# Layer 1's q and k turned by DMA in two 16-bit planes instead of on TensorE

## The chip, the cores and the metric

The kernel runs on one core of a Trainium2 chip. The metric is the time of one execution on the device in microseconds. A core has TensorE (PE: matmuls, and transposes as matmuls with an identity), VectorE (DVE), ScalarE (ACT), GpSimd (POOL), SyncE (SP), which here does nothing but issue DMAs, and 16 DMA engines. TensorE reads its operands from the on-chip memory SBUF and writes to the eight banks of PSUM; ScalarE and VectorE bring results from there into SBUF. Each engine runs its own instructions strictly in their order and waits at semaphores for the others.

## The reference

A decoder of two layers over 256 tokens with 2048 features in 32-bit floats. Each layer adds a mixer and a SwiGLU network (hidden size 5632) to the residual, each behind an RMS norm; a last norm ends it. Layer 0's mixer is sliding-window attention beside an mLSTM; layer 1's is forgetting attention with 16 heads of 128, and the change lies there:

```python
def forgetting_attention_mixer(xn, w_in, b_f, w_out):
    proj = xn @ w_in
    q, k, v, f = split_cols(proj, FOX_SIZES)
    ...
    log_f = jax.nn.log_sigmoid(f.astype(jnp.float32) + b_f.astype(jnp.float32))
    c = jnp.transpose(jnp.cumsum(log_f, axis=1), (0, 2, 1))
    ...
        s = jnp.einsum('bhqd,bhkd->bhqk', qb, k, preferred_element_type=jnp.float32) * scale
        s = s + cb[..., None] - c[:, :, None, :]
        s = jnp.where(pb[:, None] >= k_pos[None, :], s, -jnp.inf)
        p = jax.nn.softmax(s, axis=-1)
        return jnp.einsum('bhqk,bhkd->bhqd', p.astype(v.dtype), v)
    ...
    return out @ w_out
```

## The kernel before

**Projections.** Products keep 32-bit accuracy by splitting: each 32-bit value is a rounded part `hi` and a remainder `lo`, and three matmuls (hi·hi, lo·hi, hi·lo; L192 to L194) add up in PSUM. The activations lie split and transposed in SBUF (`xh`, `xl`: 16 blocks of 128 features by 256 tokens). The weights come in chunks of 256 rows by 512 columns (512 KB): SP loads a chunk into one of four `raw` buffers (L105), ScalarE rounds it into one of six `hi` buffers (L161), VectorE subtracts into one of six `lo` buffers (L162), and TensorE runs 12 matmuls on it. `project` (through `gemm`) walks the eight chunks of 512 output columns and leaves two PSUM banks, one for each block of 128 tokens (`acc`).

**Layer 1's attention** treats the 16 heads in four groups of four (`for i in range(4)`). For each group it projects q, then k, then v. Behind each projection `nat1` (L865) scales the two banks by the norm's factor into an SBUF tile of tokens by features (`qk`, one buffer, for q and k; `vn` for v). The scores need q and k the other way round, features on the partitions. So `transpose_many` turns the eight 128x128 blocks of a q or a k on TensorE, four to a PSUM bank (tile `ptm`, L306), and VectorE copies each bank into `qt` or `kt` (L307). Then `attention` runs: scores (L316, L323), bias and mask on VectorE, the exponentials on ScalarE (L345), the transposes of the weights (L366, L370), and the products with v (L374, L375).

**Order.** A planner simulates the program and lays down each engine's order, with the program's order as priority; so the matmuls of the next projection fill the time in which a softmax runs on the other engines. Work that is to be issued late goes into the list `later` as a pair of a step and a function: `gemm` calls `run_due` after the split of each chunk, with the chunk's number as the step, and what is due is issued there, on ScalarE behind that chunk's `hi` cast (`issue_after`).

**Turning by DMA.** The kernel has this step in two places already. A DMA transpose takes 16-bit elements, so the lower and the upper halves of the 32-bit words are copied apart by ScalarE into two planes, each plane is turned by two DMA transposes (one for each block of 128 tokens, 128 by 512 elements) from the SP queue, and two ScalarE copies put the halves together again: `split_turned` for the residual (planes L272, transposes L274, joins L279) and the end of a block of the FFN (L521, L523, L528), whose join is due some chunks later.

Of the kernel before, what the change touches and what calls it, by code (L numbers as in the profile page):

```python
# [10 lines left out]
U16 = mybir.dt.uint16  # L11
# [6 lines left out]
P = 128  # L18
D = 2048
S = 256  # L20
NT = S // P
KT = D // P
FF = 5632
NB = 512
# [15 lines left out]
}  # L40
MID = 6
MID_DOWN = 5
LATER = (6, 10)
LATER_DOWN = (5, 6)
RAWS = 4
# [10 lines left out]
def trunk(  # L56
# [20 lines left out]
    nc = tc.nc  # L77
# [89 lines left out]
    def new_acc():  # L167
        return [pa.tile([P, NB], F32, tag="acc", name="acc") for _ in range(NT)]

    later = []  # L170
# [6 lines left out]
    def gemm(acc, lhs, w, c0, n, k_from, k_to, k_all, skew=1, step=0):  # L177
        k0 = k_from
        while k0 < k_to:
            last = k_to == k_all and k0 + skew * CK >= k_all  # L180
            chunks = [load_chunk(w, kc, c0, n) for kc in range(k0, k_all if last else k0 + CK, CK)]
            run_due(later, step + k0 // CK)
            order = [(i, t) for i in range(len(chunks) * CK) for t in range(NT)]
            if last:
                order.sort(key=lambda it: it[1])
            for i, t in order:
                k = k0 + i
                hi, lo = (c[:, i % CK, 0:n] for c in chunks[i // CK])
                ah, al = lhs(k)
                ts = slice(t * P, (t + 1) * P)  # L190
                o = acc[t][:, 0:n]
                nc.tensor.matmul(o, ah[:, ts], hi, start=(k == 0), stop=False)  # L192
                nc.tensor.matmul(o, ah[:, ts], lo, start=False, stop=False)  # L193
                nc.tensor.matmul(o, al[:, ts], hi, start=False, stop=(k == k_all - 1))  # L194
            k0 += len(chunks) * CK
# [7 lines left out]
    def project(w, c0, n):  # L203
        acc = new_acc()
        gemm(acc, x_of, w, c0, n, 0, KT, KT)
        return acc
# [61 lines left out]
    def split_turned(idx, n, flat, turned, extra=None):  # L268
        planes = flat.bitcast(U16).rearrange("p (b t n) -> p b t n", b=2, t=NT)
        hu = h[:, :, n * NB : (n + 1) * NB].bitcast(U16).rearrange("p t (n b) -> p t n b", b=2)  # L270
        for b in range(2):
            nc.scalar.copy(planes[:, b, :, :], hu[:, :, :, b])  # L272
            for t in range(NT):
                nc.sync.dma_start_transpose(turned[:, b, :, t, :], planes[:, b, t, :])  # L274

        def join():
            ju = flat.bitcast(U16).rearrange("p (n b) -> p n b", b=2)
            for b in range(2):
                nc.scalar.copy(ju[:, :, b], turned[:, b, :, :, :].rearrange("p k t q -> p (k t q)"))  # L279
            split_scaled(idx, n, extra, flat.rearrange("p (k s) -> p k s", k=4))  # L280

        return join

    def scrap(fp, n):
        if n == 0:
            box = fp.tile([P, 4, NB], F32, tag="c", name="box", bufs=1)
            halves = box[:, 0:2, :], box[:, 2:4, :]
        else:
            halves = [fp.tile([P, CK, NB], F32, tag="raw", name="box", bufs=RAWS) for _ in range(2)]
        flat, turned = (a.rearrange("p a n -> p (a n)") for a in halves)  # L290
        return flat, turned.bitcast(U16).rearrange("p (b k t q) -> p b k t q", b=2, t=NT, q=P)
# [10 lines left out]
    def transpose_many(dst, srcs):  # L302
        m = len(srcs)
        pt = pm.tile([P, 4, P], F32, tag="pm", name="ptm")
        for i, s_ in enumerate(srcs):
            nc.tensor.transpose(pt[:, i, :], s_, ident)  # L306
        nc.vector.tensor_copy(dst, pt[:, 0:m, :])  # L307
# [78 lines left out]
    def out_proj(w, idx, key, extra):  # L386
        last = KT - 4
        for n0 in (0, 2):
# [3 lines left out]
            for i in range(2):  # L392
                gemm(accs[i], m_of, w, (n0 + i) * NB, NB, last, KT, KT, step=6)
                add_out(accs[i], n0 + i)
                if n0 == 0:
                    later.append((LATER[i], split_turned(idx, i, *scrap(extra[2], i), extra)))
                else:
# [75 lines left out]
    def ffn(layer, fp, sx, sd, key, idx_next=None, key_next=None, finish=None):  # L473
# [6 lines left out]
        for g0, g1 in zip(PARTS, PARTS[1:]):  # L480
# [4 lines left out]
            for g in range(g0, g1):  # L485
# [58 lines left out]

                todo = [(MID if g < g1 - 1 else MID_DOWN, join)]

# [314 lines left out]
    with tc.tile_pool(name="od", bufs=1) as od:  # L861
        def nat1(acc, n, name, bufs=1):
            t_ = od.tile([P, NT, n], F32, tag=name, name=name, bufs=bufs)
            for t in range(NT):
                nc.scalar.mul(t_[:, t, :], acc[t][:, 0:n], r1[:, t : t + 1])  # L865
            return t_

        VT = 2 * FD
        c_v = 2 * FOX_H * FD
        acc = project(wi1, c_v + 14 * FD, VT + FOX_H)  # L870
        fg = od.tile([P, NT, FOX_H], F32, name="fg")
        for t in range(NT):
            nc.vector.scalar_tensor_tensor(
                out=fg[:, t, :],
                in0=acc[t][:, VT : VT + FOX_H],
                scalar=r1[:, t : t + 1],
                in1=bias_f,
                op0=ALU.mult,
                op1=ALU.add,
            )  # L880
        vtail = nat1(acc, VT, "vtail")
        nl = od.tile([P, NT, FOX_H], F32, name="nl")
        nc.scalar.activation(nl, fg, AF.Abs)
        nc.scalar.activation(nl, nl, AF.Exp, scale=-1.0)
        nc.scalar.activation(nl, nl, AF.Ln, bias=1.0)
        nc.vector.scalar_tensor_tensor(out=nl, in0=fg, scalar=0.0, in1=nl, op0=ALU.min, op1=ALU.subtract)
        nc.vector.tensor_scalar(nl, nl, -1.0, None, op0=ALU.mult)
        pc = pm.tile([P, NB], F32, tag="pm", name="pcf")
        nc.tensor.matmul(pc[:, 0:FOX_H], upper, nl[:, 0, :], start=True, stop=True)
        nc.tensor.matmul(pc[:, FOX_H : 2 * FOX_H], ones, nl[:, 0, :], start=True, stop=False)  # L890
        nc.tensor.matmul(pc[:, FOX_H : 2 * FOX_H], upper, nl[:, 1, :], start=False, stop=True)
        negc = od.tile([P, NT, FOX_H], F32, name="negc")
        nc.vector.tensor_copy(negc.rearrange("p t h -> p (t h)"), pc[:, 0 : 2 * FOX_H])
        pr = pm.tile([P, NB], F32, tag="pm", name="prf")
        nc.tensor.matmul(pr[0:FOX_H, 0:P], nl[:, 0, :], upper, start=True, stop=True)
        nc.tensor.matmul(pr[0:FOX_H, P:S], nl[:, 0, :], ones, start=True, stop=False)
        nc.tensor.matmul(pr[0:FOX_H, P:S], nl[:, 1, :], upper, start=False, stop=True)
        negct = od.tile([FOX_H, S], F32, name="negct")
        nc.vector.tensor_copy(negct, pr[0:FOX_H, 0:S])
        scratch = dp.tile([FOX_H, S], F32, name="scratch")  # L900
        nc.gpsimd.dma_start(scratch, negct)
        cb1 = od.tile([P, FOX_H, S], F32, name="cb1")
        nc.gpsimd.dma_start(cb1, scratch.partition_broadcast(P))
        cb0 = od.tile([P, FOX_H, P], F32, name="cb0")
        for dst, src in ((cb0, cb1[:, :, 0:P]), (cb1[:, :, P:S], cb1[:, :, P:S])):
            nc.gpsimd.affine_select(
                out=dst, in_=src, pattern=[[0, FOX_H], [-1, P]], compare_op=ALU.is_ge, fill=NEG, base=0, channel_multiplier=1
            )

        for i in range(4):  # L910
            qt = od.tile([P, 4, S], F32, tag="qt", name="qtf")
            kt = od.tile([P, 4, S], F32, tag="kt", name="ktf")
            for off, dst in ((0, qt), (FOX_H * FD, kt)):
                n_ = nat1(project(wi1, off + i * NB, NB), NB, "qk")
                for g in range(0, 4, 2):
                    transpose_many(
                        dst[:, g : g + 2, :].rearrange("p g (t q) -> p (g t) q", q=P),
                        [n_[:, t, (g + u) * FD : (g + u + 1) * FD] for u in range(2) for t in range(NT)],
                    )
            vn = nat1(project(wi1, c_v + i * NB, NB if i < 3 else VT), NB if i < 3 else VT, "vn")  # L920

            def v_of(j, b, i=i, vn=vn):
                if i == 3 and j >= 2:
                    return vtail[:, b, (j - 2) * FD : (j - 1) * FD]
                return vn[:, b, j * FD : (j + 1) * FD]

            attention(
                od,
                lambda j, b, qt=qt: qt[:, j, b * P : (b + 1) * P],
                lambda j, kt=kt: kt[:, j, :],  # L930
                v_of,
                FD,
                FD**-0.5,
                cb0[:, 4 * i : 4 * i + 4, :],
                cb1[:, 4 * i : 4 * i + 4, :],
                4 * i,
                negc=negc[:, :, 4 * i : 4 * i + 4],
            )
# [76 lines left out]
```

## Time and profile before

| | |
|---|---|
| median of 3 runs | 2132.01 us (2131.75 to 2132.25) |
| the profiled execution | 2131.7 us |
| its span, first to last instruction | 2130.0 us |
| TensorE matmuls busy | 2113.6 us (99%) |
| VectorE busy | 1666.1 us (78%) |
| ScalarE busy | 1256.1 us (59%) |
| DMA, hardware queue of SP | 61.5% of 16 engines' time |
| granted TensorE clock, mean | 0.998 |

The profile comes from one execution. An engine's busy time is the union of its instructions; matmuls overlap in the pipeline, so the row of a group gives a matmul's length, and the distance between the starts of two neighbours gives what one costs. A group's row reads: line, engine, operation, the tile written and the tiles read, shape, count, then total and mean time and the idle time before it with what ended it. In a row of one line or tile the durations are shortest, median and longest in ns, then the first and the last start in us. In a row of the order of time the first number is the start, the second the length. `PEld` is TensorE's weight load, `SPq` an instruction in SP's queue.

### The profile page before, as it was taken

What the parts mean: (1) busy time and instruction counts of PE and PEld (TensorE: products, weight loads), DVE (VectorE), ACT (ScalarE), POOL (GpSimd) and SP (SyncE); (2) the same over time, 40 slices, a digit from 0 to 9 for tenths busy, and PEclk for the clock granted to TensorE, in tenths of its full rate; (3) what the DMA queues carried; (4) which work ended last, traced back from release to release, by engine and by line L of the source; (5) the groups of instructions that cost most, each with busy time, mean ns of one, the idle gap of its engine ahead of it and who ended that gap; (6) DMA issues with size and microseconds to landing.
All of it is one profiled execution on the core that took longest, in us unless ns stands there. A gap on an engine that the chain in (4) does not pass through costs nothing.

```text
span 2130.0 us, 26773 instructions
## 1 busy us (share of the span) xinstructions
PE 2113.6 (99%) x9732; PEld 1755.0 (82%) x9732; DVE 1666.1 (78%) x2116; ACT 1256.1 (59%) x1584; POOL 39.6 (2%) x61
## 2 busy tenths in 40 slices
PE   8999999999999999999999999999999999999998
PEld 7888888888888888888888888888888888888886
DVE  6665558998899988998755554579998998889984
ACT  6565457765567646666645544576654667556753
POOL 2010000000000000000010000000000000000000
PEclk9999999999999999999999999999999999999999
DMA  8444547665667666766575564675756666656763
GB/s 268 149 150 148 169 150 265 217 208 197 198 207 225 211 207 193 235 206 198 163 235 168 168 178 142 195 247 187 238 188 208 207 208 206 228 189 208 228 200 125
DMA packets 267941, 421.47 MB, mean 198 GB/s; under 512 B 67136, under 2 KB 75424, under 8 KB 267552
## 3 DMA queue, kind: packets, MB, share of 16 engines
q1 hardware_dynamic: 267136, 416.02, 61.5%
q0 software_dynamic: 624, 3.72, 0.5%
q8 instruction: 76, 1.25, 0.2%
q14 instruction: 57, 0.47, 0.1%
q10 hardware_dynamic: 48, 0.02, 0.0%
HBM read 404.48 MB, written 2.11 MB: 191 GB/s over the span
## 4 chain that ended last, share of the span: by engine, by line
PE 98%; ACT 1%; issue 0%; DMA 0%; DVE 0%; DVEq 0%; POOLq 0%; POOL 0%; ACTq 0%
PE acc L402 17%; PE acc L403 17%; PE acc L404 17%; PE acc L192 10%; PE acc L193 10%; PE acc L194 10%; PE prod L402 4%; PE prod L404 4%; PE prod L403 4%; PE p L323 1%; PE ptm L306 1%; PE po L374 1%; PE pt L245 0%; PE pp L366 0%; PE p L316 0%
## 5 line engine op out<-in xcount | busy, mean ns | idle before, releaser
L161 ACT CAST hi<-raw 128x1024 fp32r<-128x1024 f32 (+1 forms) x692 | 705.1, 1033 | 667.3 <-PE acc L404 314.4
L162 DVE TENSOR_TENSOR lo<-raw,hi 128x1024 fp32r<-128x1024 f32 (+1 forms) x692 | 821.5, 1200 | 314.7 <-ACT hi L161 312.9
L403 PE MATMUL acc<-lo,xh 128*128 128x512 f32 x946 | 368.1, 389 | 0.0
L404 PE MATMUL acc<-hi,xl 128*128 128x512 f32 x946 | 367.2, 389 | 0.0
L402 PE MATMUL acc<-hi,xh 128*128 128x512 f32 x946 | 366.5, 389 | 0.0
L192 PE MATMUL acc<-hi,xh 128*128 128x512 f32 (+3 forms) x736 | 276.7, 377 | 0.8 <-ACT hi L161 0.8
L194 PE MATMUL acc<-hi,xl 128*128 128x512 f32 (+3 forms) x736 | 276.8, 377 | 0.0
L193 PE MATMUL acc<-lo,xh 128*128 128x512 f32 (+3 forms) x736 | 276.3, 375 | 0.0
L404 PEld LDWEIGHTS acc<-hi,xl 128*128 128x128 f32 x946 | 177.6, 188 | 36.9
L403 PEld LDWEIGHTS acc<-lo,xh 128*128 128x128 f32 x946 | 177.6, 188 | 36.7
L402 PEld LDWEIGHTS acc<-hi,xh 128*128 128x128 f32 x946 | 177.6, 188 | 36.6
L295 DVE TENSOR_TENSOR lt<-t,ht 128x1024 fp32r<-128x1024 f32 x168 | 199.7, 1217 | 3.6 <-ACT ht L294 3.6
L403 PE MATMUL acc<-lo,mh 128*128 128x512 f32 x514 | 200.2, 389 | 0.0
L402 PE MATMUL acc<-hi,mh 128*128 128x512 f32 x514 | 200.0, 389 | 0.0
L404 PE MATMUL acc<-hi,ml 128*128 128x512 f32 x514 | 198.5, 389 | 0.0
L294 ACT CAST ht<-t 128x1024 fp32r<-128x1024 f32 x168 | 174.8, 1052 | 20.8 <-PE acc L404 12.8
L192 PEld LDWEIGHTS acc<-hi,xh 128*128 128x128 f32 x736 | 139.0, 189 | 25.0 <-ACT hi L161 1.2
L194 PEld LDWEIGHTS acc<-hi,xl 128*128 128x128 f32 x736 | 139.1, 189 | 24.4 <-issue 0.8
L193 PEld LDWEIGHTS acc<-lo,xh 128*128 128x128 f32 x736 | 139.2, 189 | 24.0 <-issue 0.7
L192 PE MATMUL acc<-hi,mh 128*128 128x512 f32 x320 | 125.2, 391 | 1.2 <-ACT mh L294 1.2
L193 PE MATMUL acc<-lo,mh 128*128 128x512 f32 x320 | 125.3, 392 | 0.0
L194 PE MATMUL acc<-hi,ml 128*128 128x512 f32 x320 | 123.9, 390 | 0.0
(311 smaller groups left out, 2779.4 us busy)
## 6 DMA issues: line engine op xcount, KB each, us to landing
raw<-in_w_gate_dram SPq DMA_DIRECT2D x176, 512.0 KB, 4.3
raw<-in_w_up_dram SPq DMA_DIRECT2D x176, 512.0 KB, 4.6
raw<-in_w_down_dram SPq DMA_DIRECT2D x176, 512.0 KB, 4.6
raw<-in_w_in_odd_dram SPq DMA_DIRECT2D x88, 512.0 KB, 3.8
raw<-in_w_in_even_dram SPq DMA_DIRECT2D x64, 512.0 KB, 4.0
raw<-in_w_out_even_dram SPq DMA_DIRECT2D x32, 512.0 KB, 3.6
raw<-in_w_out_odd_dram SPq DMA_DIRECT2D x32, 512.0 KB, 4.2
raw<-in_w_in_odd_dram SPq DMA_DIRECT2D x8, 272.0 KB, 2.9
```

The lines of the kernel that those rows point to most:

```text
L161: latest[0] = nc.scalar.copy(hi[:, :, 0:n], raw[:, :, 0:n])
L162: nc.vector.tensor_tensor(out=lo[:, :, 0:n], in0=raw[:, :, 0:n], in1=hi[:, :, 0:n].bitcast(F32), op=ALU.subtract)
L192: nc.tensor.matmul(o, ah[:, ts], hi, start=(k == 0), stop=False)
L193: nc.tensor.matmul(o, ah[:, ts], lo, start=False, stop=False)
L194: nc.tensor.matmul(o, al[:, ts], hi, start=False, stop=(k == k_all - 1))
L294: nc.scalar.copy(dst_h, src)
L295: nc.vector.tensor_tensor(out=dst_l, in0=src, in1=dst_h.bitcast(F32), op=ALU.subtract)
L306: nc.tensor.transpose(pt[:, i, :], s_, ident)
L323: nc.tensor.matmul(p1[:, jj, :], q_of(j, 1), k_of(j), start=True, stop=True)
L402: nc.tensor.matmul(o, ah, hi, start=start, stop=False)
L403: nc.tensor.matmul(o, ah, lo, start=False, stop=False)
L404: nc.tensor.matmul(o, al, hi, start=False, stop=stop)
```

## The change

For the groups 0, 1 and 2, q and k are turned by the DMA step: the new function `turn` copies the two planes of the `qk` tile on ScalarE, issues four DMA transposes on SP, and returns a function `join`, which copies the two turned planes into `qt` or `kt` on ScalarE. The join is put into `later` with step 6 (`AHEAD`): for a q it is issued behind the cast of the seventh chunk of the k projection, for a k behind that of the seventh chunk of the v projection. Group 3 keeps its transposes on TensorE. `planes` and `turned` are new tiles with one buffer each, 4 KB a partition each.

```diff
+AHEAD = 6
...
+        def turn(src, dst):
+            planes = od.tile([P, 2, NT, NB], U16, tag="planes", name="planes")
+            turned = od.tile([P, 2, 4, NT, P], U16, tag="turned", name="turned")
+            su = src.bitcast(U16).rearrange("p t (n b) -> p t n b", b=2)
+            for b in range(2):
+                nc.scalar.copy(planes[:, b, :, :], su[:, :, :, b])
+                for t in range(NT):
+                    nc.sync.dma_start_transpose(turned[:, b, :, t, :], planes[:, b, t, :])
+
+            def join():
+                du = dst.rearrange("p k s -> p (k s)").bitcast(U16).rearrange("p (n b) -> p n b", b=2)
+                for b in range(2):
+                    nc.scalar.copy(du[:, :, b], turned[:, b, :, :, :].rearrange("p k t q -> p (k t q)"))
+
+            return join
+
         for i in range(4):
             qt = od.tile([P, 4, S], F32, tag="qt", name="qtf")
             kt = od.tile([P, 4, S], F32, tag="kt", name="ktf")
             for off, dst in ((0, qt), (FOX_H * FD, kt)):
                 n_ = nat1(project(wi1, off + i * NB, NB), NB, "qk")
+                if i < 3:
+                    later.append((AHEAD, turn(n_, dst)))
+                    continue
                 for g in range(0, 4, 2):
                     transpose_many(
```

## The prediction

> **What bounds the kernel now.** I read the page first (span, busy shares, the chain that ended last), then the stage of layer 1 that is edited, in windows of one head group each, then who waits for whom there.
>
> ```profile
> span 2130.0 us, 26773 instructions
> PE 2113.6 (99%) x9732; PEld 1755.0 (82%) x9732; DVE 1666.1 (78%) x2116; ACT 1256.1 (59%) x1584; POOL 39.6 (2%) x61
> PE 98%; ACT 1%; issue 0%; DMA 0%; DVE 0%; DVEq 0%; POOLq 0%; POOL 0%; ACTq 0%
> ```
>
> TensorE is busy for 99% of the span, and 98% of the chain of work that ended last is its own. The windows below are the three head groups that the change touches; each begins where the q of a group is nearly projected.
>
> ```profile
> core 0: us, PE busy (x) PEld busy (x) DVE busy (x) ACT busy (x) POOL busy (x), PEclk, DMA share, GB/s
> 1075.00:1149.00 74.00, 74.00 (x351) 61.79 (x350) 41.68 (x48) 36.28 (x52) 4.95 (x2) 1.00 0.64 202
> 1149.00:1223.00 74.00, 74.00 (x350) 61.82 (x349) 40.01 (x48) 34.85 (x51) 0.00 (x0) 1.00 0.57 171
> 1223.00:1297.00 74.00, 74.00 (x350) 61.77 (x350) 40.00 (x48) 34.84 (x51) 0.00 (x0) 1.00 0.57 171
> ```
>
> The reader is to see that TensorE has no hole at all here (74.00 of 74.00), at the full granted clock, while ScalarE is busy for 35 to 36 us of 74, VectorE for 40 to 42 and the DMA engines for 0.57 to 0.64 of the time. So what leaves TensorE shortens the kernel one for one, and what is laid on the others costs nothing until TensorE has to wait for it. The waits of 1075 to 1297 us, ScalarE's and then the SP queue's, show how far that is:
>
> ```profile
> ACT hi L161 <- PE acc L194: 94.4, 53, 3.8
> ACT hi L161 <- DMA raw<-in_w_in_odd_dram: 2.1, 2, 1.8
> ...
> SPq L105 <- DVE lo L162: 174.6, 69, 6.6
> ```
>
> ScalarE waits 94.4 us for TensorE to give back weight buffers, and the load queue waits 174.6 of 222 us for the split: the supply of weights runs ahead and is held back by TensorE.
>
> **What is removed.** Six projections (q and k of groups 0 to 2) lose eight 128x128 transposes each, and VectorE two 128x512 copies each. First the rows of the transposes in 1075 to 1300 us, then the order of time on TensorE around the first eight (start, length):
>
> ```profile
> L306 PE MATMUL ptm<-ident,qk x48: 270/272/273, 1081.2 to 1253.4; 128*128 128x128 f32 x48
> ...
> L307 DVE COPY ktf<-ptm x8: 679/690/692, 1105.6 to 1326.6; 128x512 f32<-128x512 f32 x8
> ```
>
> ```profile
> 1079.88 0.39 PE L194 MATMUL acc<-hi,xl 128*128 128x512 f32 x1
> ...
> 1081.25 0.38 PE L306 MATMUL ptm<-ident,qk 128*128 128x128 f32 x2
> ...
> 1082.40 0.82 PE L306 MATMUL ptm<-ident,qk 128*128 128x128 f32 x6
> ...
> 1083.52 0.39 PE L194 MATMUL acc<-hi,xl 128*128 128x512 f32 x1
> ...
> 1084.68 0.39 PE L193 MATMUL acc<-lo,xh 128*128 128x512 f32 x1
> ...
> 1089.66 0.39 PE L194 MATMUL acc<-hi,xl 128*128 128x512 f32 x1
> ```
>
> A transpose lasts 272 ns by its own row, but they overlap, so the price is read from starts. From 1083.52 to 1089.66 there are 27 matmul steps and nothing else: 6.14 / 27 = 0.227 us a step. From 1079.88 to 1084.68 there are 17 such steps and the eight transposes: 4.80 - 17 x 0.227 = 0.94 us, or 0.118 a transpose. Six times that is **5.6 us** off TensorE. Bounds: the six in one piece end 0.82 us after the first start, of which 0.27 is the tail of the last, so 0.11 apart and 48 x 0.11 = 5.3 us at the least; the whole 0.272 each would give 13.1 us, but a start-to-start reading contradicts it. I take 5.6. The twelve VectorE copies (12 x 0.69 = 8.3 us) are worth nothing, as nothing late waits for VectorE here.
>
> **What is added.** Each of the six turns gets two ScalarE copies that take the 16-bit halves apart, four DMA transposes on the SP queue, and two ScalarE copies that join the halves, placed behind the seventh weight cast of the next projection. The kernel has the same step elsewhere; its rows (the residual's turn, then one turn of the FFN in order of time, on ScalarE and on the SP queue):
>
> ```profile
> L274 SPq DMA_TRANSPOSE box<-box x20: 1200/1262/1891, 305.1 to 1392.3; - x20
> L272 ACT COPY box<-h x10: 1031/1042/1047, 304.0 to 1386.9; 128x1024 uint16<-128x1024 uint16 x10
> L279 ACT COPY box<-box x10: 1335/1352/1366, 312.5 to 1401.4; 128x1024 uint16<-128x1024 uint16 x10
> ...
> DMA to landing us min/median/max: 2.4/2.5/4.2
> ```
>
> ```profile
> 1480.45 1.99 ACT L521 COPY c<-c 128x1024 uint16<-128x1024 uint16 x2
> ...
> 1489.69 1.06 ACT L161 CAST hi<-raw 128x1024 fp32r<-128x1024 f32 x1 [1.71 <-PE acc L404]
> 1490.64 2.58 ACT L528 COPY c<-turned 128x1024 uint16<-128x1024 uint16 x2
> ...
> 1481.51 5.14 SPq L523 DMA_TRANSPOSE turned<-c  x4
> ```
>
> *ScalarE*: 1.99 + 2.58 = 4.6 us a turn, 27 us in all, into 222 - 106 = 116 us that are idle. *SP queue*: 5.14 us a turn, 31 us in all, beside 174.6 us of waiting. *From the first plane copy to the end of the join*: 1.06 us until the first transpose issues, 5.14 - 1.26 = 3.9 until the fourth does, 2.5 until it lands, then 2.6 for the join: 10.1 us. Where this stands, for the k of group 0, and the first use of a k (POOL's queue has no part in it):
>
> ```profile
> 1100.29 0.69 ACT L865 ACTIVATE qk<-acc,r 128x512 f32<-128x512 f32 x1 [0.67 <-PE acc L194]
> 1100.88 1.04 ACT L161 CAST hi<-raw 128x1024 fp32r<-128x1024 f32 x1
> 1103.01 1.05 ACT L161 CAST hi<-raw 128x1024 fp32r<-128x1024 f32 x1 [1.09 <-PE acc L194]
> 1106.65 1.05 ACT L161 CAST hi<-raw 128x1024 fp32r<-128x1024 f32 x1 [2.58 <-PE acc L194]
> ```
>
> ```profile
> 1104.10 1.22 DVE L162 TENSOR_TENSOR lo<-raw,hi 128x1024 fp32r<-128x1024 f32 x1 [0.92 <-ACT hi L161]
> ...
> L316 PE MATMUL p<-ktf,qtf x32: 271/275/275, 1122.8 to 1335.7; 128*128 128x128 f32 x32
> ...
> raw<-in_w_in_odd_dram SPq DMA_DIRECT2D x88, 512.0 KB, 3.8
> ```
>
> The plane copies can start at 1101.0, or at 1101.9 behind one cast; the fourth transpose has landed by 1109.4 and the join ends at 1112.0. The first scores read k at 1122.8, by then some 1.9 us earlier (two turns less): **9 us of room**. A q has a whole projection more.
>
> The new waits, and what stands behind each. (1) On ScalarE the join waits for the landing, with the weight casts behind it. The cast at 1103.01 is the seventh of its projection, because six buffers let casts run six chunks ahead; placed straight behind it, the join would hold ScalarE from 1104.06 to 1112.0, and the next cast, now at 1106.65, would be 5.4 us late. A chunk is 12 x 0.227 = 2.72 us of TensorE; a chunk cast at 1103.01 is split by 1105.32, 2.3 us later, and used five chunks after that cast's start, 13.6 us: a lead of **11.3 us**. So 5.4 is covered, with 5.9 to spare, and made up in four chunks, since a cast of 1.05 leaves 1.67 us in each. In the FFN row above, casts were put between the planes and the join and the join waited for nothing; I expect the same here. (2) On the SP queue the first transpose waits for the plane copy and the loads stand behind it: 1.06 + 5.14 = 6.2 us at most. A load goes out four buffers ahead, 4 x 2.72 = 10.9 us, and lands in 3.8: 7.1 us to spare, and behind that the 11.3. (3) The DMA engines take 8 x 128 KB = 1 MB more in 74 us, 14 GB/s on 171 to 202. (4) The two new tiles have one buffer each: the planes of a k wait for the transposes of its q, which landed more than 10 us before, and on ScalarE the next `qk` tile waits only for ScalarE's own plane copies. All four cost nothing as long as these leads stand; beyond them each microsecond costs TensorE one.
>
> **Sum.** Removed 5.6, added 0 on the path. The profiled execution lasted 2131.7 us (span 2130.0), so 2126.1, with a span of 2124.4; it lies 0.3 below the median of the runs, 2132.0, so **2126.4** against that, 0.26% faster. A difference of 0.2%, 4.3 us, is about what a measurement of this kernel can tell from no change, so only 1.3 us stand between this and "the same".
>
> **Rivals.**
> *Part is given back.* The planner orders all engines anew around the new instructions, and TensorE takes its orders in turn: a transpose of the softmax or a score put a little too early waits. For it: the longest landing, 4.2 us, is 1.7 over the median, and the joins of the FFN did wait, as the group of that line shows:
>
> ```profile
>   DMA turned<-c: 2.4, 5
> ```
>
> That is 0.5 us at a time. Against it: ScalarE's wait is not TensorE's, and TensorE had no hole in these windows. From 0.25 to 1.6 us a turn, 1.5 to 9.8 in all, the kernel lies between 2127.9 and 2136; at 0.7 a turn 2130.6.
>
> *Slower: the join holds the casts.* If the transposes land more than 5.9 us later than reckoned while the join stands first on ScalarE, TensorE runs out of weights in each of the six turns; from 7.6 us on (six times 1.65, the 5.6 and 4.3 together) the kernel is slower by 0.2%. Were the four transposes to land one after another, each in its longest 4.2 us, that would be 16.8 us where I put 6.4: 10.4 late, 4.5 of it uncovered, 27 in all, 2153. At the median 2.5 in series it is 10.0, 3.6 late, and still covered. The turn in the FFN speaks against it: from the first issue at 1481.51 the join began at 1490.64, and a cast stood in between.
>
> The Trainium skill, "VectorE: DVE Perf Modes", section "The three transpose paths", puts a 128x128 16-bit transpose at 390 ns on TensorE and 1309 ns by DMA, and its "Rules for kernel authors" say to use TensorE if PSUM will do as the destination, which speaks against this change. By its figure the 16 blocks of a turn are an estimated 20.9 us, 14.5 late, 8.6 uncovered, and 2178 us. The trace differs on both: four DMA transposes of four blocks each issued in 5.14 us, 0.32 a block, and TensorE paid 0.118 for a 32-bit block.
>
> *More is gained.* VectorE, the PSUM banks and TensorE's order become freer. Nothing waits for them in these windows, so this would be tenths: below 2125.5.
>
> **How the numbers follow.** The forecast 0.66 (its own range 2125.5 to 2127.7), more gained 0.04, part given back 0.18, the held casts 0.12. Faster by over 0.2% (below 2127.7) is 0.70, within 0.2% 0.18, slower 0.12. The range of 8 in 10 goes from 2125.0 to 2133.0: it leaves out the held casts, the upper end of the part given back (0.05) and the very lowest.
>
> **What would show it.** In the changed profile: 16 transposes of `qk` in place of 64; windows of the three groups without a hole on TensorE and each about 1.9 us shorter; 24 more DMA transposes, landing in 2.5 us; the join of a k ended some 9 us before the first score matmul reads it; no wait of TensorE for a cast, a split or a join. The prediction is wrong if a wait of TensorE's weight loads for ScalarE or VectorE appears in these windows, if the fourth transpose of a turn lands more than 12 us after the first was issued, or if TensorE's steps of 0.227 us stretch while transposes are in flight.

## The result

| | before | after |
|---|---|---|
| median, 7 runs each | 2131.47 us (2130.54 to 2132.25) | 2125.33 us (2124.65 to 2126.20) |
| ratio, 95% interval | | 0.9971 (0.9962 to 0.9981) |
| span of the profiled execution | 2130.0 us | 2123.7 us |

The kernel is 0.29% faster, between 0.19% and 0.38%. Of the changed kernel's page, the lines that answer to those of before:

```profile
span 2123.7 us, 26736 instructions
PE 2107.4 (99%) x9684; PEld 1749.7 (82%) x9684; DVE 1657.1 (78%) x2104; ACT 1281.8 (60%) x1608; POOL 40.6 (2%) x61
PE 98%; ACT 1%; issue 0%; DMA 0%; DVE 0%; DVEq 0%; POOLq 0%; POOL 0%; ACTq 0%
```

TensorE has 48 instructions and 6.2 us less, ScalarE 24 copies and 25.7 us more; TensorE is still the whole chain. Where the time went is read from the first score of each of the groups 0 to 2, before (first fence) and after (second), in the order of time on TensorE:

```profile
1122.80 0.61 PE L316 MATMUL p<-ktf,qtf 128*128 128x128 f32 x4
...
1196.66 0.61 PE L316 MATMUL p<-ktf,qtf 128*128 128x128 f32 x4
...
1270.52 0.61 PE L316 MATMUL p<-ktf,qtf 128*128 128x128 f32 x4
```

```profile
1120.63 0.61 PE L317 MATMUL p<-ktf,qtf 128*128 128x128 f32 x4
...
1192.61 0.61 PE L317 MATMUL p<-ktf,qtf 128*128 128x128 f32 x4
...
1264.58 0.61 PE L317 MATMUL p<-ktf,qtf 128*128 128x128 f32 x4
```

From one group to the next it was 73.86 us and is 71.98 and 71.97: 1.88 or 1.89 less, two turns at 0.94. Three groups make 5.6 of the 6.3 us by which the spans differ. The rest lies outside the edited stage: 0.3 ahead of group 0 and 0.4 in the last microseconds, behind TensorE's last matmul. The windows of the three groups after the change, one period each:

```profile
1075.00:1147.00 72.00, 72.00 (x333) 60.13 (x333) 38.02 (x44) 44.60 (x60) 4.95 (x2) 1.00 0.69 219
1147.00:1219.00 72.00, 72.00 (x333) 60.12 (x333) 37.45 (x44) 43.41 (x59) 0.00 (x0) 1.00 0.63 190
1219.00:1291.00 72.00, 72.00 (x334) 60.12 (x333) 37.44 (x44) 43.43 (x59) 0.00 (x0) 1.00 0.63 190
```

TensorE still has no hole, while ScalarE went from 35 to 43 us a group. What is left of the transposes is seen in the rows of the tile `qk`, and the added work in those of `turned` in layer 1:

```profile
L307 PE MATMUL ptm<-ident,qk x16: 271/272/273, 1296.9 to 1319.5; 128*128 128x128 f32 x16
```

```profile
L918 SPq DMA_TRANSPOSE turned<-planes x24: 1197/1266/1953, 1081.7 to 1249.5; - x24
...
  DMA turned<-planes: 3.9, 6
...
DMA to landing us min/median/max: 2.3/2.4/4.2
```

Sixteen transposes remain, all of group 3, and the 24 DMA transposes landed 2.4 us after their issue. The waits of ScalarE and of the SP queue from 1075 to 1291 us (total, times, longest):

```profile
ACT hi L162 <- PE acc L195: 46.8, 33, 3.8
ACT hi L162 <- DMA raw<-in_w_in_odd_dram: 14.7, 12, 2.0
```

```profile
SPq L106 <- DVE lo L163: 112.6, 50, 6.6
SPq L918 <- ACT planes L916: 22.5, 6, 5.2
```

ScalarE's wait for buffers that TensorE gives back has halved (94.4 to 46.8 us), and now it waits 14.7 us for weights that are late: the lead shrank, but it did not run out.

### The profile page after: what moved, and what is told of

It is laid out like the page before. It is cut to its first block, busy times and chain, and to the rows that moved or that the text cites. A ratio compares the mean times of both kernels' runs of the same rounds, so it can differ in the third digit from the quotient of the medians.

```text
span 2123.7 us, 26736 instructions
## 1 busy us (share of the span) xinstructions
PE 2107.4 (99%) x9684; PEld 1749.7 (82%) x9684; DVE 1657.1 (78%) x2104; ACT 1281.8 (60%) x1608; POOL 40.6 (2%) x61
## 4 chain that ended last, share of the span: by engine, by line
PE 98%; ACT 1%; issue 0%; DMA 0%; DVE 0%; DVEq 0%; POOLq 0%; POOL 0%; ACTq 0%
PE acc L404 17%; PE acc L403 17%; PE acc L405 17%; PE acc L193 10%; PE acc L195 10%; PE acc L194 10%; PE prod L404 4%; PE prod L403 4%; PE prod L405 4%; PE p L324 1%; PE po L375 1%; PE pt L246 0%; PE ptm L307 0%; PE pp L367 0%; PE p L317 0%
```

## The experiments

### Removed alone, added alone

The transposes taken away with nothing but a VectorE copy of the same size in their place (this kernel leaves out the turning, so its scores are not the reference's), and the DMA step put beside the transposes:

```diff
                 if i < 3:
-                    later.append((AHEAD, turn(n_, dst)))
+                    nc.vector.tensor_copy(dst..., n_...)
                     continue
```

> The transposes of q and k of groups 0 to 2 are left out and nothing is put in their place but one VectorE copy of the same size (the scores are then those of unturned tiles, so this part of the computation is not the reference's). Theory: the whole gain of the change is the 48 transposes that left TensorE, 5.6 us, and the work added is hidden. So this kernel is as fast as the changed one within 1 us, about 2126, and each of the three groups is 1.9 us shorter from first score to first score. Rival: the added copies and DMAs cost TensorE something. Then this kernel is faster than the changed one by that amount, over 1 us.

```diff
                 if i < 3:
                     later.append((AHEAD, turn(n_, dst)))
-                    continue
```

> Groups 0 to 2 keep their transposes on TensorE and are turned by DMA as well; the join writes the same values into the same tiles once more. Theory: the added 27 us of ScalarE, 31 us of the SP queue and 24 DMA transposes are covered, so the time is that of the kernel before, 2131.5 within 1 us, with no wait of TensorE in the three groups. Rival: they have a price of their own that the removed transposes more than paid for. Then the time is over that of before by more than 1 us.

Removed alone: 2125.64 us, 0.9975 of before (0.9965 to 0.9984), 0.3 from the changed kernel, and its first scores of the three groups are 71.99 and 71.96 us apart, as the changed kernel's are. Added alone: 2130.74 us, 0.9998 (0.9990 to 1.0007), 0.4 below before, which is inside its interval. The windows of added alone:

```profile
1075.00:1149.00 74.00, 74.00 (x351) 61.79 (x350) 40.05 (x49) 44.51 (x60) 5.45 (x2) 1.00 0.70 209
1149.00:1223.00 74.00, 74.00 (x350) 61.82 (x349) 39.96 (x49) 43.17 (x58) 0.00 (x0) 1.00 0.63 185
```

TensorE runs the same 351 and 350 instructions in the same 74 us as before, with ScalarE 8 us a group busier beside it. So the gain is the removed transposes, and the added work costs nothing that these runs resolve.

### More turns: the q of the last group, and its k

```diff
-                if i < 3:
+                if i < 3 or off == 0:      # e4
+                if i < 4:                  # e3
```

> Only the q of group 3 is turned by DMA besides; its join falls into the k projection, which is 512 columns wide as those of the groups before. Theory: 8 more transposes at 0.118 us, 0.94 us less than the changed kernel, about 2124.4, with no wait. Rival, that the end of the stage is set by something else: no difference from the changed kernel.

> Group 3 is turned by DMA too, 16 more transposes off TensorE. If only the count matters: 1.9 us less than the changed kernel, about 2123.5. By the leads: group 3's v projection is 256 columns wide, its eight chunks take about 12 us in place of 22, and the turn of k takes 10 us from the first plane copy and starts 1 to 2 us after the projection ends. So the first scores of group 3 have between +1 and -2 us of room, the q's 0.9 us are gained and the k's 0.9 are lost again in a wait of up to 2 us: 2124 to 2126, and the profile shows TensorE waiting once, before the first score of group 3.

With the q: 2124.21 us, 0.9969 (0.9956 to 0.9981). With both: 2123.76 us, 0.9966 (0.9952 to 0.9979). Each step has the sign and about the size of eight transposes (1.1 and 0.5 us less), though the intervals overlap. What I expected of the k, that TensorE would wait before the first score of group 3, did not happen. The end of the k's join, and TensorE there, with all four groups turned:

```profile
1323.69 1.37 ACT L923 COPY ktf<-turned 128x1024 uint16<-128x1024 uint16 x1 [0.33 <-DMA turned<-planes]
```

```profile
1326.21 0.28 PE L195 MATMUL acc<-hi,xl 128*128 128x256 f32 x1
1326.33 0.40 PE L193 MATMUL acc<-hi,mh 128*128 128x512 f32 x1
...
1327.26 0.40 PE L194 MATMUL acc<-lo,mh 128*128 128x512 f32 x1
1327.50 0.60 PE L317 MATMUL p<-ktf,qtf 128*128 128x128 f32 x4
```

The join ended at 1325.06, 1.2 us before the last matmul of v started, so the k was not late: there was room at the upper end of the +1 to -2 us that I gave it. Between that matmul (1326.21) and the first score (1327.50) stand five matmuls of the output projection, 1.2 us of other work, where in the changed kernel the score follows v directly (1327.97, 1328.09). That the planner put them there because it reckoned with a later k is likely but not shown.

### Twice the transposes, and three and four times

Each transpose of a turn preceded by one, two or three spare ones into a spare tile (e5, e10, e6):

```diff
                 for t in range(NT):
+                    for _ in range(1):       # e5; 2 in e10, 3 in e6
+                        nc.sync.dma_start_transpose(spare[:, :, t, :], planes[:, b, t, :])
                     nc.sync.dma_start_transpose(turned[:, b, :, t, :], planes[:, b, t, :])
```

> The changed kernel with each DMA transpose of the six turns issued once more ahead of it, into a spare tile: eight instead of four a turn. Theory of leads: the SP queue is held some 10 us a turn, against 7.1 us by which the loads and 11.3 by which the casts run ahead; the last transpose lands near 1113 us, the join of the first k ends near 1116 and its first score is due at 1120.6. All covered: 2125.3 within 1 us and no wait of TensorE in the groups. Rival, that transposes in flight slow TensorE or the loads: over 2126.5.

> Three spare transposes ahead of each of the four, all of one block into the same place, so that each waits for the landing of the one before: some 8.5 us for each block of 128 by 512, 34 us a turn. The k of a group is then there some 17 us after its first score is due. If the loads stand behind the transposes in the SP queue all that time, the leads (7.1 + 11.3 = 18.4 us) are used up and TensorE waits about 15 us in each of the six turns: up to 2215. If the planner lays loads between them and puts other matmuls ahead of the late scores, the price is small: 2125 to 2130.

> Two spare transposes ahead of each of the four, twelve a turn. In the run with sixteen, the loads of the first turn went out 23 us late and TensorE waited 6.7 us, so 16.3 were covered; four transposes fewer at 1.3 us make it some 18 late and 1 to 2 us of waiting for a q, and 4 to 7 for a k, whose turn follows before the lead is built up again: 15 to 27 us in all, 2140 to 2152, with ScalarE waiting for weights. If landing and not the queue were what counts, the first scores would be late and nothing else: about 2126.

Eight a turn: 2126.84 us, 0.9979 (0.9970 to 0.9989). Twelve: 2169.20, 1.0178 (1.0161 to 1.0195). Sixteen: 2193.52, 1.0293 (1.0276 to 1.0311). The two with more lose tens of us, while eight cost about 1.5 us against the changed kernel. That is more than the 2125.3 within 1 us that I expected and in the range of the rival, over 2126.5, though the intervals of the two kernels overlap. The SP queue in the first turn with sixteen, and then TensorE there:

```profile
1076.78 0.37 SPq L106 DMA_DIRECT2D raw<-in_w_in_odd_dram  x1
1079.76 1.20 SPq L920 DMA_TRANSPOSE spare<-planes  x1
...
1101.25 1.25 SPq L920 DMA_TRANSPOSE spare<-planes  x1
1102.55 2.12 SPq L106 DMA_DIRECT2D raw<-in_w_in_odd_dram  x4
```

```profile
1101.21 0.39 PE L195 MATMUL acc<-hi,xl 128*128 128x512 f32 x1
1108.17 1.22 PE L193 MATMUL acc<-hi,xh 128*128 128x512 f32 x2 [6.57 <-ACT hi L162]
```

The load that was due one chunk after 1076.78, at 1079.5, goes out at 1102.55, 23.0 us late. TensorE's next step starts 6.96 us after the last one instead of 0.227: 6.7 us of waiting, so 16.3 of the 23.0 were covered. I had reckoned 18.4 (7.1 and 11.3). The sixteen were issued in 22.7 us, so they did not wait for one another's landing, as my 34 us a turn supposed. With twelve the q's wait was about as forecast (1.05 us for the cast in group 0), but a k, whose turn follows before the lead is restored, cost more than the 4 to 7 us I gave it, and the 2140 to 2152 expected was missed by 17 us: the waits of TensorE with twelve and with sixteen are

```profile
PE acc L193 <- ACT hi L162: 30.6, 5, 10.4
```

```profile
PE acc L193 <- ACT hi L162: 49.6, 6, 11.3
```

and those sums alone don't reach the 44 and 68 us lost against the changed kernel. The granted clock of these two was 0.990 and 0.984, against 0.998; what that costs is shown further down, on a kernel where it can be told from the waits.

The eight of e5 gave times from 2124.4 to 2130.0, where the changed kernel's lie within 1.6 us. The same kernel once more:

> The kernel with eight transposes a turn once more: its times spread from 2124.4 to 2130.0 us, where the changed kernel's spread over 1.6, and its profile was of the shortest. If the spread is the lead running out by chance, a profile of one of the longer executions, 2127 or more, shows TensorE waiting for a cast in one or two of the k's turns, with the granted clock halved for a few us behind it. If it shows no wait, the cause lies elsewhere. If the profiled execution is again a short one, it stays open.

It gave 2126.82 us (0.9979, 0.9968 to 0.9991), the same median again, and the profile is of an execution of 2127.97. In the groups it shows waits, but not for a cast:

```profile
PE pp L367 <- DVE s L359: 1.1, 2, 1.0
```

The transposes of the softmax weights stand in TensorE's order where the planner expects VectorE to be done, and VectorE was 1 us late. The first profile, of an execution of 2124.43, has no such wait, and as both hold the same matmuls in the same order, their starts can be compared one by one: of the 3.6 us between their spans (2122.7 and 2126.3) the longer execution loses 1.4 at these transposes in group 0 and 0.7 in group 2. The other 1.4 arose in layer 0 and are shown in the last section. The second half of group 0's k is joined as follows, in the shorter execution and then in the longer:

```profile
1114.31 1.36 ACT L926 COPY ktf<-turned 128x1024 uint16<-128x1024 uint16 x1 [3.82 <-DMA turned<-planes]
```

```profile
1117.52 1.35 ACT L926 COPY ktf<-turned 128x1024 uint16<-128x1024 uint16 x1 [3.81 <-DMA turned<-planes]
```

The join is 3.2 us later where TensorE is 1.4 later, and the softmax behind it 3.6 (its first exponential at 1133.19 against 1129.58). The lag begins in the q's turn at a cast that waits 1.0 us for a weight load and does not wait in the shorter execution; why that load was late stays open, and so does how much each of the two differences has in the spread of all 18 runs.

### Holding ScalarE

Copies of the residual onto itself, written ahead of the join: two (e7), four (e8), and four with the next cast bound behind them (e11).

```diff
             def join():
+                for _ in range(4):           # 2 in e7
+                    nc.scalar.copy(h..., h...)   # e11 keeps the last one as held[0]
...
+        # e11 alone, in split_chunk:
+            with tc.issue_after(held[0].ins):
+                latest[0] = nc.scalar.copy(hi[:, :, 0:n], raw[:, :, 0:n])
```

> The changed kernel with ScalarE held ahead of each join by two copies of the residual onto itself (128x4096, values unchanged), some 7 us. Theory: weight casts are 11.3 us ahead of TensorE; with the join's 2.7 the cast behind it is some 8 to 9 us late, so no wait: 2125.3 within 1 us. Rival, that the lead is shorter than I read it: several us more, with TensorE waiting for a split in each turn.

> The same with four such copies, some 14 us, ahead of each of the six joins. The cast behind is some 16 us late against a lead of 11.3: TensorE waits 4 to 5 us in each turn, 25 to 30 in all, about 2150 to 2155, and the first scores come later too. If the planner puts the casts ahead of the held copies, or the lead is longer than I read it: near 2125.

> The four held copies and the join again, and now the next weight cast is put behind the last of them in ScalarE's order, so that the planner can lay no cast between: ScalarE is kept from casting for 4 x 3.6 + 2.6 = 17 us in each turn. The next cast, due some 2 us after the hold begins, is 15 us late. With the lead of 11.3 us as I read it, TensorE waits 3 to 5 us in each of six turns, 20 to 28 in all: 2145 to 2153, with TensorE waiting for a cast or a split. If the lead is longer than that: near 2125.

Two: 2124.88 us, 0.9970 (0.9959 to 0.9982). Four: 2124.94, 0.9972 (0.9961 to 0.9983), so no price where I expected 25 to 30 us. ScalarE in the q of group 0 with four:

```profile
1083.27 3.62 ACT L922 COPY h<-h 128x4096 f32<-128x4096 f32 x1
1086.80 1.04 ACT L162 CAST hi<-raw 128x1024 fp32r<-128x1024 f32 x1
1087.74 1.35 ACT L925 COPY qtf<-turned 128x1024 uint16<-128x1024 uint16 x1
...
1091.13 3.62 ACT L922 COPY h<-h 128x4096 f32<-128x4096 f32 x1
```

The planner laid the casts between the copies, and here the join ahead of all copies but the first, so this did not hold ScalarE in one piece and says nothing of the lead. It says that 14.5 us more of ScalarE's work a turn fits in. Bound in order, four cost 2164.28 us, 1.0154 (1.0138 to 1.0169). ScalarE and TensorE in the first of these turns:

```profile
1083.08 1.04 ACT L164 CAST hi<-raw 128x1024 fp32r<-128x1024 f32 x1
1084.03 3.62 ACT L928 COPY h<-h 128x4096 f32<-128x4096 f32 x1
...
1100.78 1.04 ACT L167 CAST hi<-raw 128x1024 fp32r<-128x1024 f32 x1
```

```profile
1096.46 0.39 PE L201 MATMUL acc<-hi,xl 128*128 128x512 f32 x1
1101.87 1.10 PE L199 MATMUL acc<-hi,xh 128*128 128x512 f32 x2 [5.01 <-ACT hi L167]
```

```profile
PE acc L199 <- ACT hi L167: 26.3, 6, 5.0
```

From the start of the hold at 1084.03 TensorE worked on until 1096.7, 12.7 us, where I had reckoned 13.6 from the start of a cast to its use. Of the 2.3 us that I took off for cast and split only the cast's 1.04 counted: TensorE started at 1101.87, as the cast ended (1101.82). So a cast could be 11.6 us late in this turn, beside my 11.3. TensorE then waited 5.2 us; its six waits for that cast sum to 26.3 us, in the range of 20 to 28 that I gave. But the kernel lost 39 and missed the 2145 to 2153 expected, so the price of a wait was larger than the wait.

### One more turn elsewhere

All four groups, and the q of layer 0's mLSTM:

```diff
-            for g in range(0, ML_H, 2):
-                transpose_many(qmt..., [qm...])
+            later.append((AHEAD, turn(qm, qmt, mp)))
```

> All four groups of layer 1, as before, and the q of layer 0's mLSTM (eight transposes of a 256x512 tile, whose products stand behind the k projection) turned by DMA. Theory: 8 more transposes at 0.118 us, 0.9 us less than with the four groups alone, about 2122.8, no wait of TensorE. Rival: layer 0's ScalarE and VectorE have less room around the gates, and a wait takes the 0.9 us back: 2123.8 or more.

2123.37 us, 0.9962 (0.9949 to 0.9976): the fastest of these kernels, by 0.4 us in the medians over the four groups alone, where 0.9 was expected, and their ranges overlap (2122.02 to 2123.85, 2123.52 to 2124.23), so it does not decide between the gain and the rival that takes it back. In its groups TensorE waits for nothing.

## Why the prediction was right

The forecast was 2126.4 us, 5.6 below the median shown then; measured are 2125.33 and a difference of 6.1. That lies in the range, but 0.2 us under the forecast's own part of it, where 0.04 was given to "more gained". The rival's mechanism is not what brought it there: the groups gave the 5.6 forecast, half of the 1.1 us between forecast and median is that the kernel before itself came out 0.5 lower this time (2131.47 against 2132.01), and the other half is of the size of the 0.3 and 0.4 outside the edited stage. As far as the runs show, these 1.1 us are chance and no merit of the mechanism. The mechanism held; two sizes, the path of a turn and the hold of the SP queue, were off, as follows.

**The price of a transpose.** 0.94 us for eight, read from starts: the groups became 1.88 and 1.89 us shorter, two turns each. The time of a single transpose by its row, 272 ns, would have given 13 us. This term was right to within what the trace resolves.

**That the added work costs nothing.** Shown by added alone, at 0.9998 of before with an unbroken TensorE. Of the signs that would have spoken against the prediction none appeared: no wait of TensorE for a cast, a split or a join in the groups, landings at most 4.2 us behind their issue, and matmul steps of 0.227 us with transposes in flight as without.

**The path of a turn.** 10.1 us from the first plane copy to the end of the join; the k of group 0 took 8.9, by ScalarE's order of time:

```profile
1100.59 1.99 ACT L916 COPY planes<-qk 128x1024 uint16<-128x1024 uint16 x2
...
1105.45 1.38 ACT L923 COPY ktf<-turned 128x1024 uint16<-128x1024 uint16 x1
1107.22 1.05 ACT L162 CAST hi<-raw 128x1024 fp32r<-128x1024 f32 x1 [0.39 <-PE acc L195]
1108.17 1.36 ACT L923 COPY ktf<-turned 128x1024 uint16<-128x1024 uint16 x1
```

It ended at 1109.53, 11 us ahead of the first score at 1120.63, where I had 9. It is shorter because the planner joined the first plane while the second was still in flight. For the same reason the step "the join waits for nothing" failed in the small: ScalarE waited for a landing in six of the copies, 3.9 us in all, behind which the casts stood, and none was late for TensorE.

**What the SP queue is held.** I put it at 6.2 us at most against 7.1 to spare. Measured, the first transpose of a turn alone waited up to 5.2 us for its planes (22.5 us in six), and then come the four transposes with 5.1, 10.3 together; so the loads did use up their own lead, and ScalarE waited 14.7 us for them. This term was too small, and the casts' lead behind it covered the difference.

**The leads.** The casts' 13.6 and 11.3 us were 12.7 and 11.6 in the one turn read in order; the 18.4 for loads was 16.3. The point from which the held casts decide, some 6 to 8 us later than reckoned, has the right order: four spare transposes (5.1 us more) brought no wait for a cast in the groups, eight (some 10 us more) did. What I had not seen is that the planner moves the casts and the join around added work, as the four unbound copies showed, and the first score with them (1127.83 there, 1120.63 in the changed kernel). Work that it could lay out this way cost nothing here; work bound in one piece, and a queue filled with transposes, did.

**The rivals.** "Part is given back" named a softmax transpose put a little too early. It did not occur in the changed kernel and did occur with the transposes doubled, where the longer execution lost 2.1 us to it. By the figure of the Trainium skill in "VectorE: DVE Perf Modes", section "The three transpose paths", the held casts would have made it 2178 us; the trace does not agree, with four DMA transposes in 5.1 us of the SP queue (1101.7 to 1106.8 in the k of group 0) and landings of 2.4. That page's rule, under "Rules for kernel authors", to use TensorE if PSUM will do, did not hold for this kernel, which TensorE bounds throughout.

## What to carry to other kernels

Price what leaves the bounding engine by the distance between starts, not by the length of one instruction, and multiply: here 48 transposes were 5.6 us, small but clear of the interval. Then ask for the lead of each queue that the added work is put on, in microseconds of the bounding engine's work, and compare it with the longest piece that can stand there unbroken; totals of idle time don't answer that. Adding alone and removing alone, one kernel each, settle whether a gain is the removed part.

## What the runs showed of the hardware

In these runs a wait of TensorE cost more than its length. With ScalarE held in order, the windows before the first wait (1096.7 to 1101.9), right behind it and later (the number after the busy times is the granted clock):

```profile
1089.00:1096.00 7.00, 7.00 (x32) 5.81 (x31) 0.00 (x0) 6.97 (x3) 0.00 (x0) 1.00 0.44 146
...
1102.00:1105.40 3.40, 3.40 (x8) 2.36 (x9) 3.40 (x4) 2.66 (x3) 0.00 (x0) 0.50 0.34 72
1106.00:1112.00 6.00, 6.00 (x28) 4.97 (x27) 2.55 (x3) 3.56 (x5) 0.00 (x0) 1.00 0.98 311
```

After 5 us without work the clock is granted at 0.50 for 3.4 us, in which 8 matmuls start where 15 would. Over the span:

```profile
core 0: 2164.2 us, clock 0.993
```

against 0.998 in the changed kernel. The difference, 0.005 of 2164 us, is some 10.8 us (2 more or less, by the rounding of the two clocks), and with the 26.3 of waiting it makes about 37 of the 40.5 us between the two profiled spans. The Trainium skill, "TensorE: Matmul & The Clock Gate", section "Part 1: The HAM clock gate (the "warmup" mystery)", gives half the clock after an idle window of about 3.4 us, until such a window has been busy; the trace agrees, with 3.4 us at 0.50 behind a wait of 5.0.

The clock was halved without any wait as well. In layer 0, around the mLSTM's gates, the two profiles of the kernel with eight transposes a turn differ (first the longer execution, then the shorter):

```profile
186.00:190.00 4.00, 4.00 (x24) 3.35 (x24) 2.50 (x12) 0.94 (x4) 0.00 (x0) 1.00 0.66 210
190.00:194.00 4.00, 4.00 (x14) 3.21 (x13) 2.31 (x4) 2.77 (x7) 0.00 (x0) 0.57 0.00 0
```

```profile
186.00:190.00 4.00, 4.00 (x24) 3.10 (x23) 2.49 (x10) 0.60 (x3) 0.00 (x0) 1.00 0.78 251
190.00:194.00 4.00, 4.00 (x25) 3.35 (x23) 2.31 (x5) 3.11 (x9) 0.00 (x0) 1.00 0.01 3
```

TensorE is busy throughout in both, with the same transposes, small matmuls and projection, and yet one execution gets 0.57 of the clock in the second window and starts 14 instructions, where the other starts 25 at the full clock. The 0.43 of 4 us that are missing are 1.7 us, and the starts agree: the longer execution is 0.3 us ahead before these windows (a matmul at 189.72 against 190.05) and 1.3 behind after them (195.19 against 193.92). That is nearly all of the 1.4 us that arise ahead of layer 1's groups. It comes from a stage that no edit of theirs touched and is nearly as much as two turns, so differences of this size are safer read from a stage's own rows than from the whole time. The profiles of before and of the changed kernel both have the halved clock at this place (0.57 from 190 to 194 us; 0.83 and 0.74 from 186 to 194), so the 6.3 us between their spans don't come from it. Why it comes in some executions and not in others stays open.
